# First row tiles of three feed-forward networks as block products, two opened side by side

## The chip, the cores and the metric

The kernel runs on one core of one Trainium2 chip. The metric is the device time of one execution in microseconds (us), the median of several. The engines are TensorE (PE; its weight loads are listed as PEld and overlap the matmuls), VectorE (DVE), ScalarE (ACT), GpSimd (POOL) and SyncE (SP). Matrix products land in PSUM banks; everything else lies in on-chip tiles that DMA fills from memory. SP issues plain loads; POOL issues DMAs that add to what is already in the tile ("accumulate").

## The reference

A trunk of two layers over 512 frames and 16 meta tokens, 528 columns of 1024 channels in float32. Each layer has a feed-forward network, a mixer (attention and a convolution branch), and a second feed-forward network:

```python
def swiglu(x, w_gate, w_up, w_down):
    return (jax.nn.silu(x @ w_gate) * (x @ w_up)) @ w_down

for l in range(DEPTH):                       # DEPTH = 2, D_MODEL = 1024, D_FF = 2816
    h = h + 0.5 * swiglu(rmsnorm(h, ffn1_norm[l]), ffn1_w_gate[l], ffn1_w_up[l], ffn1_w_down[l])
    h = h + hybrid_mixer(rmsnorm(h, mix_norm[l]), ...)
    h = h + 0.5 * swiglu(rmsnorm(h, ffn2_norm[l]), ffn2_w_gate[l], ffn2_w_up[l], ffn2_w_down[l])
return rmsnorm(h, final_norm)[:, N_META:]
```

So there are four feed-forward networks, called here (layer, which): (0,0), (0,1), (1,0), (1,1). In each, gate and up are 22 row tiles of 128 channels.

## The kernel before

**Precision.** Each float32 operand is split into a high part (a cast) and a low part (the rest); a product is three matmuls: high x high, high weight x low, low weight x high. `split` (L76 to L80) does it: a ScalarE copy and a VectorE subtraction. For the mixer's weights (`MIXER`, L223 to L226) the low part is made otherwise: ScalarE writes -1 times the high part, and a POOL DMA accumulates the weight on it.

**Columns.** The 528 columns are two halves of 264. A *plain* tile (L492) computes one row tile of gate or of up: 8 channel tiles, 3 products, 2 halves, 48 matmuls.

**Block products.** `quad` (L566) computes two row tiles, m and m+1, of gate and up together. Weights are 2 by 2 blocks of channels and row tiles, the input 2 by 2 blocks of channels and column halves; seven block products of 24 matmuls take the place of eight. Four use sums of weight blocks: s1 = w11 + w12, s3 = w22 + w12, s2 = s1 + w22, s4 = s2 + w21 (s2 and s4 are added up in s1's tile); the other three use w11, w21 and w22 as they are. Their order is `QUAD` (L109). In it ScalarE copies the w11 product to a second bank (B) and the s1 product to a tile q, s2 adds into B, VectorE writes "the opposite" q - B to a bank E (L608), w21 finishes the first result, s3 adds into B, VectorE writes q - B again (c22), w22 finishes E, s4 finishes B. A result leaves in three steps: VectorE times the norm, ScalarE's Silu, VectorE times up; then `parts` splits it to ah and al for the down products. Sums of the input (sh, sl) are made by `sums` (L365).

**A network** (L467) begins with its *head* (L517): plain tiles of gate and up for m = 0, then m = 1, with the matmuls of the RMS norm and the last sums of the input after 12 matmuls of the second. Then come a quad for m = 2, 3, the first down products, more quads, and so on (`GROUPS`). The network (0,0) has its own head with four plain rows. Heads begin at 730.48, 1087.56 and 1793.79 us.

**Weights.** `units` (L130) lists them in the order of use. Each is loaded by SP into one of three buffers wr (`fetch`, L179), then made to a high and a low part wh and wl (four buffers each) three units ahead of its use (`LOOK`, `prep_unit`, L213). Block sums s1 and s3 are loaded by SP and completed by a POOL accumulate of w12, in two buffers each (`fetch_sums`, L196).

**Order.** Each engine works through its own queue in order. The framework's scheduler sets that order from the program's text and from priorities; code in `priority(n)` is moved, and a manual dependency puts one instruction behind another.

## Time and profile before

| | |
|---|---|
| time, median of 3 runs | 2152.31 us (2151.03 to 2152.36) |
| profiled execution, first to last instruction | 2150.5 us |
| TensorE busy | 2135.9 us (99%) |
| VectorE, ScalarE, GpSimd busy | 1521.5, 1137.9, 488.7 us |
| the SP queue, the accumulating queue | 226.36 MB, 95.44 MB |
| granted TensorE clock, mean | 0.999 |
| the 192 matmuls and 4 of the norm in head (1,0) | 1087.56 to 1111.43 us |

The profile is that of one execution. A row of a timeline has the start, the duration, the engine, the line of the program, the operation with its output and inputs by the program's names, and in brackets how long the engine had been idle before it and what released it. The chain follows the work that ended last back to its beginning; "PE pb L502 x48" there is 48 matmuls of line 502 into a tile pb.

### The profile page before, as it was taken

Reading aid. Unit: us, or ns where it says so; the run is one execution under the profiler, and the core shown is the slowest. Engines: PE = TensorE matmul, PEld = TensorE weight load, DVE = VectorE, ACT = ScalarE, POOL = GpSimd, SP = SyncE. Lnnn points to the kernel's source line nnn. Section 1 sums busy time; section 2 is a strip of 40 time slices with the busy share of each in tenths; the row PEclk is TensorE's granted clock in tenths of the full one; section 3 lists DMA queues with packets and bytes.
Section 4 is the critical chain, followed back from the end, with each engine's and each line's share of the span. In section 5 each row is a group of like instructions: output and inputs, shape, how many; then the busy total and the mean of one; then the engine's idle time right before and its main releaser. Section 6 shows DMA issues by size and latency. Waiting matters only on the chain.

```text
span 2150.5 us, 39932 instructions
## 1 busy us (share of the span) xinstructions
PE 2135.9 (99%) x16226; PEld 2052.8 (95%) x16226; DVE 1521.5 (71%) x2091; ACT 1137.9 (53%) x1587; POOL 488.7 (23%) x449
## 2 busy tenths in 40 slices
PE   9999999999999999999999999999999999999998
PEld 9999999999999999999999999999888889999897
DVE  7867685677766777677877676856677767767685
ACT  6434355467776545343554443554778775444354
POOL 1322321211111131313113223212112111322320
PEclk9999999999999999999999999999999999999999
DMA  8465536865578747464365655368656886665542
GB/s 236 133 165 141 142 104 198 181 138 119 134 169 180 175 129 189 129 161 122 99 169 145 168 140 146 103 193 184 142 127 133 187 188 167 159 175 143 144 111 77
DMA packets 140168, 324.90 MB, mean 151 GB/s; under 512 B 15568, under 2 KB 19664, under 8 KB 139984
## 3 DMA queue, kind: packets, MB, share of 16 engines
q1 hardware_dynamic: 101856, 226.36, 33.3%
q0 software_dynamic: 37440, 95.44, 26.1%
q8 instruction: 127, 2.08, 0.4%
q10 hardware_dynamic: 688, 0.55, 0.1%
q14 instruction: 57, 0.47, 0.1%
HBM read 315.86 MB, written 6.42 MB: 150 GB/s over the span
## 4 chain that ended last, share of the span: by engine, by line
PE 99%; ACT 0%; DVE 0%; DMA 0%; issue 0%; DVEq 0%; ACTq 0%
PE pb L580 16%; PE ps L580 16%; PE ps L720 15%; PE ps L260 12%; PE ps L706 10%; PE pe L260 6%; PE pb L260 6%; PE pe L580 5%; PE z L706 2%; PE ps L502 2%; PE pe L502 1%; PE pb L502 1%; PE z L877 1%; PE po L921 1%; PE z L900 1%; PE ps L554 1%
## 5 line engine op out<-in xcount | busy, mean ns | idle before, releaser
L79 ACT CAST wh<-wr 128x1024 fp32r<-128x1024 f32 (+4 forms) x275 | 242.2, 887 | 372.4 <-PE ps L260 94.5
L80 DVE TENSOR_TENSOR wl<-wr,wh 128x1024 fp32r<-128x1024 f32 (+4 forms) x275 | 300.6, 1096 | 57.4 <-ACT wh L79 53.5
L79 ACT CAST wh<-s 128x1024 fp32r<-128x1024 f32 x158 | 165.8, 1049 | 274.9 <-DVE s L236 83.1
L80 DVE TENSOR_TENSOR wl<-s,wh 128x1024 fp32r<-128x1024 f32 x158 | 216.1, 1368 | 59.4 <-ACT wh L79 58.7
L720 PE MATMUL ps<-uh,wh 128*128 128x264 f32 (+1 forms) x792 | 243.8, 308 | 0.0
L720 PE MATMUL ps<-uh,wl 128*128 128x264 f32 (+1 forms) x792 | 240.0, 303 | 0.0
L720 PE MATMUL ps<-ul,wh 128*128 128x264 f32 (+1 forms) x792 | 239.9, 303 | 0.0
L640 POOL TENSOR_TENSOR h<-h,dt 128x528 f32<-128x528 f32 (+1 forms) x96 | 179.9, 1879 | 258.1 <-DVE dt L638 255.2
L210 POOL DMA_DIRECT2D s<-wg x78 | 72.8, 938 | 596.9 <-DMA s<-wg 337.9
L748 DVE SCALAR_TENSOR_TENSOR y<-uc,prm,y 128x528 f32<-128x528 f32 (+1 forms) x240 | 197.7, 824 | 4.1
L224 ACT CAST wh<-wr 128x1024 fp32r<-128x1024 f32 x104 | 109.1, 1049 | 141.2 <-issue 46.9
L580 PE MATMUL ps<-ul,wh 128*128 128x264 f32 (+1 forms) x624 | 177.4, 284 | 0.0
L580 PE MATMUL pb<-sl,wh 128*128 128x264 f32 (+1 forms) x624 | 176.9, 283 | 0.0
L580 PE MATMUL ps<-uh,wl 128*128 128x264 f32 (+1 forms) x624 | 176.9, 283 | 0.0
L580 PE MATMUL pb<-sh,wl 128*128 128x264 f32 (+1 forms) x624 | 176.8, 283 | 0.0
L580 PE MATMUL pb<-sh,wh 128*128 128x264 f32 (+1 forms) x624 | 176.5, 283 | 0.0
L580 PE MATMUL ps<-uh,wh 128*128 128x264 f32 (+1 forms) x624 | 176.2, 282 | 0.0
L720 PEld LDWEIGHTS ps<-uh,wl 128*128 128x128 f32 x792 | 149.1, 188 | 5.9
L720 PEld LDWEIGHTS ps<-uh,wh 128*128 128x128 f32 x792 | 148.9, 188 | 5.4
L720 PEld LDWEIGHTS ps<-ul,wh 128*128 128x128 f32 x792 | 149.0, 188 | 5.1
L260 PE MATMUL ps<-ah,wh 128*128 128x264 f32 (+1 forms) x616 | 142.0, 300 | 0.0
L260 PE MATMUL ps<-ah,wl 128*128 128x264 f32 (+1 forms) x616 | 141.8, 300 | 0.0
(319 smaller groups left out, 6460.8 us busy)
## 6 DMA issues: line engine op xcount, KB each, us to landing
wr<-wd SPq DMA_DIRECT2D x96, 384.0 KB, 3.6
wr<-win SPq DMA_DIRECT2D x72, 512.0 KB, 4.4
wl<-win POOLq DMA_DIRECT2D x72, 512.0 KB, 7.8
wr<-wg SPq DMA_DIRECT2D x117, 256.0 KB, 3.0
wr<-wu SPq DMA_DIRECT2D x117, 256.0 KB, 3.4
s<-wg SPq DMA_DIRECT2D x78, 256.0 KB, 5.2
s<-wu SPq DMA_DIRECT2D x78, 256.0 KB, 5.7
s<-wg POOLq DMA_DIRECT2D x78, 256.0 KB, 5.2
```

The source lines that it names most:

```text
L79: act.copy(hi, x)
L80: dve.tensor_tensor(out=lo, in0=x, in1=f(hi), op=ALU.subtract)
L210: pool.dma_start(t[:, a:b], src, accum_op=ALU.add)
L224: act.copy(hi[:, :nk], raw[:, :nk])
L260: pe.matmul(ps[:, c, :n], wt[:, k0 + k, :], xt[:, s:s + n], start=(k == 0 and pi == 0), stop=(k == end and pi == 2))
L502: pe.matmul(ps[:, e, :TH], wt[:, k, :], xt[:, s], start=(k == ORDER[0] and pi == 0), stop=(k == ORDER[-1] and pi == 2))
L554: pe.matmul(ps[:, e, :TH], wt[:, k, :], xt[:, s], start=(k == 0 and pi == 0), stop=(k == KD - 1 and pi == 2))
L580: pe.matmul(ps[:, e, :TH], wt[:, 4 * e + kk, :], xt, start=start and kk == 0 and pi == 0, stop=kk == 3 and pi == 2, skip_group_check=True)
L640: pool.tensor_tensor(out=tri(h[j], mode), in0=tri(h[j], mode), in1=tri(t, mode), op=ALU.add)
L706: pe.matmul(ps, wt[:, k0 + k, :], xt[:, s], start=(n == 0 and pi == 0), stop=(n == nk - 1 and pi == 2))
L720: pe.matmul(ps, wt[:, k, :], xt[:, s], start=(n == 0 and pi == 0), stop=(n == KD - 1 and pi == 2))
L748: t = dve.scalar_tensor_tensor(out=y, in0=uc[i][:, c0 + k:k + T], scalar=col(w0 + k), in1=y, op0=ALU.mult, op1=ALU.add)
```

## The change

In the networks (0,1), (1,0) and (1,1) the plain tiles of m = 0 and 1 and the quad of m = 2 and 3 are replaced by `pair`: two block products, a for m = 0, 1 and b for m = 2, 3, side by side in the order `OPENING`. It begins with o11 of both (the product that a quad calls w11), which need no sums of the input, each with its first three channel tiles first; after them the norm's matmuls and o21a, then s1a, s2a, o21b, w22a, s3a, s1b, s4a, s2b, s3b, w22b, s4b. The order of the matmuls inside a head is as written; that of the other engines is the scheduler's, with `URGENT` for the PSUM copies. The "opposite" is done in two halves. The low parts of o11a, o11b and o21a are made as in the mixer, with a -1 copy and a POOL accumulate. s1a is loaded into a wr buffer and completed there. The network (0,0) and all quads but those three are as before, apart from `evict`, which has the same instructions as before.

```diff
+    RAW_OF = {"w11": (0, 0), "w22": (1, 1), "w12": (0, 1), "w21": (1, 0),
+              "o11": (0, 0), "o21": (1, 0)}
+    OPEN = ("o11", "o21")
+    OPENING = (("o11", 0), ("o11", 1), ("o21", 0), ("s1", 0), ("s2", 0), ("o21", 1), ("w22", 0), ("s3", 0), ("s1", 1),
+               ("s4", 0), ("s2", 1), ("s3", 1), ("w22", 1), ("s4", 1))
...
+    def open_pair(of, srcs):
+        ats = [(*of, src[2]) for src in srcs]
+        opened.update(ats)
+        return [((n, *ats[e]), srcs[e], n) for n, e in OPENING]
...
-            m = PLAIN if l or fi else PLAIN_FIRST
-            for m in range(m):
-                units += [((f"g{fi}", l, m), wg[l, m], 8), ((f"u{fi}", l, m), wu[l, m], 8)]
-            m += 1
+            if l or fi:
+                units += open_pair((fi, l), [(wg[l], wu[l], m) for m in (0, 2)])
+            else:
+                for m in range(PLAIN_FIRST):
+                    units += [((f"g{fi}", l, m), wg[l, m], 8), ((f"u{fi}", l, m), wu[l, m], 8)]
+            m = PLAIN_FIRST
...
-            fetches += [n, n + 5, n + 3]
+            later_sums.append((n, ("s1", "s3")))
+            fetches += [(n, (name, *at), name) for name in ("w11", "w22", "w21")]
+        elif nk == "s1" and at in opened:
+            first = units[n - 1][2] in OPEN
+            later_sums.append((n, ("s3",) if first else ("s1", "s3")))
+            fetches += [(n, key, nk)] if first else []
+        elif at in opened and nk in ("s2", "s4"):
+            fetches.append((n, ("w22" if nk == "s2" else "w21", *at), "w22" if nk == "s2" else "w21"))
         elif nk not in QUAD:
-            fetches.append(n)
+            fetches.append((n, key, nk))
+    def load(raw, n, *blocks):
+        for queue, block, kw in zip((nc.sync, pool), blocks, ({}, {"accum_op": ALU.add})):
+            for a, b, src in pieces(n, block):
+                queue.dma_start(raw[:, a:b], src, **kw)
...
+            load(raw, n, *(("w11", "w12") if block == "s1" else (block,)))
...
+        n, names = later_sums[min(state["sums"], len(later_sums) - 1)]
+        _, *at = units[n][0]
+        if state["sums"] == len(later_sums) or tuple(at[:2]) != quads["of"]:
             return
-        state["sums"] = n + 1
-        _, *at = units[n][0]
-        for name, first in (("s1", "w11"), ("s3", "w22")):
-            t = quads["pool"].tile([P, 8, P], F32, tag=name, bufs=2, name=name)
-            for a, b, src in pieces(n, first):
-                nc.sync.dma_start(t[:, a:b], src)
-            for a, b, src in pieces(n, "w12"):
-                pool.dma_start(t[:, a:b], src, accum_op=ALU.add)
+        state["sums"] += 1
+        for name in names:
+            bufs = 1 if name == "s1" and at[0] == 2 else 2
+            t = quads["pool"].tile([P, 8, P], F32, tag=name, bufs=bufs, name=name)
+            load(t, n, "w11" if name == "s1" else "w22", "w12")
...
-            raw = raws.pop(key)
-            if key[0] in MIXER:
+            raw, nk0, nk = raws[key], nk, 8 if nk in OPEN else nk
+            if key[0] in MIXER or nk0 == "o11" or nk0 == "o21" and units[n - 1][2] == "o11":
                 act.copy(hi[:, :nk], raw[:, :nk])
                 act.activation(lo[:, :nk], raw[:, :nk], AF.Copy, scale=-1.0)
-                pool.dma_start(lo[:, :nk], src[:, :nk].bitcast(F32R), accum_op=ALU.add)
+                for a, b, src in pieces(n):
+                    pool.dma_start(lo[:, a:b], src.bitcast(F32R), accum_op=ALU.add)
...
+            i = split(raws[("s1" if nk in ("s2", "s4") else nk, *at)], hi, lo)
+            if nk == "s3" and at in opened:
+                tc.add_manual_dep(i.ins, state["rsqrt"].ins.name, NOSYNC, reason="behind the norm")
...
+            i = split(r, hi, lo)
+            if behind:
+                tc.add_manual_dep(i.ins, behind.ins.name, NOSYNC, reason="behind the copies")
...
+    def pair(ptile, sp, st, mode, of, ats, between, take, done):
+        TH = (T if mode == FULL else SEQ) // 2
+        toks = halves(mode)
+        KH = KD // 2
+        def v(t):
+            return t[:, :, :TH]
+        def x(t, k):
+            return [tuple(p[:, toks[t]] for p in st["u"][kk + 4 * k]) for kk in range(KH)]
+        def sx(i):
+            return [tuple(p[:, i % 2] for p in st["S"][kk][i // 2]) for kk in range(KH)]
+        def products(ps, w, xs, start=False, ks=range(KH)):
+            hi, lo = w
+            for e in range(2):
+                for kk in ks:
+                    xh, xl = xs[kk]
+                    for pi, (wt, xt) in enumerate(((hi, xh), (hi, xl), (lo, xh))):
+                        pe.matmul(ps[:, e, :TH], wt[:, 4 * e + kk, :], xt, start=start and kk == 0 and pi == 0,
+                                  stop=kk == KH - 1 and pi == 2, skip_group_check=True)
+        def kept(c):
+            t = sp.tile([P, 2, TH], F32, tag="q", bufs=2, name="q")
+            with priority(-URGENT):
+                copies.append(act.copy(t, v(c)))
+            return t
+        def begin(c, t):
+            with priority(-URGENT):
+                copies.append(act.copy(v(c), t))
+        copies = []
+        def opposite(out, c, q):
+            for e in range(2):
+                with priority(-URGENT):
+                    dve.scalar_tensor_tensor(out=out[:, e, :TH], in0=c[:, e, :TH], scalar=-1.0, in1=q[:, e],
+                                             op0=ALU.mult, op1=ALU.add)
+        As = [ptile() for _ in range(2)]
+        ws = [unit("o11", *of, at) for at in ats]
+        for ks in (range(KH - 1), (KH - 1,)):
+            for A, w in zip(As, ws):
+                products(A, w, x(0, 0), True, ks)
+        Bs = [ptile("pb")]
+        begin(Bs[0], v(As[0]))
+        between(ptile("pe"), copies[0])
+        Bs.append(kept(As[1]))
+        q, E, c22 = {}, {}, {}
+        def step(name, n):
+            w = unit(name, *of, ats[n])
+            if name == "o21":
+                products(As[n], w, x(0, 1))
+                take(n, As[n], 0, 0)
+            elif name == "s1":
+                G = ptile() if n else ptile("pe")
+                products(G, w, sx(0), True)
+                q[n] = kept(G)
+            elif name == "s2":
+                if n:
+                    keep, Bs[n] = Bs[n], ptile()
+                    begin(Bs[n], keep)
+                products(Bs[n], w, sx(1))
+                E[n] = ptile("pe")
+                opposite(E[n], Bs[n], q[n])
+            elif name == "s3":
+                products(Bs[n], w, sx(2))
+                c22[n] = sp.tile([P, 2, TH], F32, tag="c22", bufs=2, name="c22")
+                opposite(c22[n], Bs[n], q[n])
+                take(n, c22[n], 1, 1)
+            elif name == "w22":
+                products(E[n], w, sx(3))
+                take(n, E[n], 1, 0)
+            else:
+                done(n, 1)
+                products(Bs[n], w, x(1, 1))
+                take(n, Bs[n], 0, 1)
+                done(n, 0)
+        for name, n in OPENING[2:]:
+            step(name, n)
...
+            def evict(g, u, c, t):
+                s = toks[t]
+                dve.tensor_tensor(out=g[:, s], in0=c[:, 0, :TH], in1=norm["r"][:, s], op=ALU.mult)
+                fn(g[:, s], g[:, s], AF.Silu)
+                dve.tensor_tensor(out=u[:, s], in0=c[:, 1, :TH], in1=g[:, s], op=ALU.mult)
...
-                pu, pn = ptile(), ptile("pe")
-                pg = plain("pb", "g", 0)
-                def between():
-                    norm["r"] = rms_rstd(fp, st, pn, mode)
-                    sums(gtile, 3, st, mode)
-                plain(pu, "u", 0, between)
-                evac(0, pg[:, :, :TH], pu[:, :, :TH])
-                pg = plain("ps", "g", 1)
-                evac(1, pg[:, :, :TH], plain("pe", "u", 1)[:, :, :TH])
+                ms = (0, 2)
+                gu = {}
+                def between(pn, behind):
+                    with priority(-URGENT):
+                        norm["r"] = rms_rstd(fp, st, pn, mode)
+                    sums(gtile, 3, st, mode, behind)
+                def take(n, c, i, t):
+                    if (n, i) not in gu:
+                        gu[n, i] = gtile(), fp.tile([P, T], F32, tag="up", bufs=3, name="up")
+                    evict(*gu[n, i], c[:, :, :TH], t)
+                def done(n, i):
+                    u = gu[n, i][1]
+                    if i:
+                        while late:
+                            parts(*late.pop())
+                        parts(u, ms[n] + 1)
+                    else:
+                        late.append((u, ms[n]))
+                with tc.manual_schedule(engines={mybir.EngineType.PE}):
+                    pair(ptile, quads["pool"], st, mode, (fi, l), ms, between, take, done)
```

TensorE, between s2 and s3 of a block product, network (0,1). Names: sh, sl sums of the input, uh, ul the input, wh, wl weights; ps, pb, pe banks. Before (s2 into pb, then the first rows of w21; 24 of these stand ahead of s3, which is again into pb):

```order
L580 MATMUL pb<-sl,wh 128x264
L580 MATMUL pb<-sh,wl 128x264
L580 MATMUL ps<-uh_8436,wh 128x264
L580 MATMUL ps<-ul_8437,wh 128x264
L580 MATMUL ps<-uh_8436,wl 128x264 [waits DVE_49]
```

With the change, at s2b and s3b:

```order
L440 MATMUL ps<-sl,wh 128x264
L440 MATMUL ps<-sh,wl 128x264
L293 MATMUL ps<-ah,wh 128x264 [waits Activation_49]
L293 MATMUL ps<-ah,wh 128x264
L293 MATMUL ps<-al,wh 128x264 [waits DVE_49]
L293 MATMUL ps<-al,wh 128x264
L440 MATMUL ps<-sh,wh 128x264 [waits DVE_49]
L440 MATMUL ps<-sl,wh 128x264
```

Between the last matmul of s2 and the first of s3 there stood 24 of w21; now there are four of a down tile (L293), and s3b's first one waits for VectorE.

VectorE at the same place: the instructions from s2's result on, before and then with the change (q - B is L608 before, L458 after):

```order
L608 SCALAR_TENSOR_TENSOR pe<-pb,q 128x2x264 [waits PE_49,Activation_49]
L80 TENSOR_TENSOR wl<-s_8902,wh 128x1024 [waits Activation_49]
L592 TENSOR_TENSOR g<-ps,rstd 128x264 [waits PE_49]
L80 TENSOR_TENSOR wl<-wr,wh 128x512 [waits DMAHW7_49,Activation_49]
L594 TENSOR_TENSOR up<-ps,g 128x264 [waits Activation_49]
```

```order
L645 TENSOR_TENSOR up<-pb,g 128x264 [waits Activation_49]
L458 SCALAR_TENSOR_TENSOR pe<-ps,q 128x264 [waits PE_49]
L81 TENSOR_TENSOR al<-up,ah 128x528 [waits Activation_49]
L458 SCALAR_TENSOR_TENSOR pe<-ps,q 128x264 [waits DVE_49]
L81 TENSOR_TENSOR wl<-wr,wh 128x512 [waits DMAHW1_49,Activation_49]
```

One instruction has become two halves, and a split (al) that waits for ScalarE stands between them. At s2a (bank pb) it is an addition of weights that waits for a load (L268).

ScalarE, from the opening of the same head to the block sums. Before (rstd is the norm, s_8902 a block sum):

```order
L79 CAST wh<-wr 128x1024 [waits DMAHW2_49,DMAHW1_49,PE_49]
L103 ACTIVATE rstd<-pe,bias 128x528 [waits PE_49]
L103 ACTIVATE rstd<-rstd,bias 128x528 [waits Activation_49]
L99 ACT_TABLE_LOAD
L79 CAST wh<-s_8902 128x1024 [waits DMASW1_49,DMASW0_49,PE_49]
L103 ACTIVATE g<-g 128x528 [waits DVE_49]
```

With the change:

```order
L80 CAST wh<-wr 128x1024 [waits DVE_49,PE_49]
L451 COPY pb<-ps 128x2x264 [waits PE_49]
L105 ACTIVATE rstd<-pe,bias 128x528 [waits PE_49]
L446 COPY q<-ps 128x528
L105 ACTIVATE rstd<-rstd,bias 128x528 [waits Activation_49]
L80 CAST sh<-g 128x528 [waits DVE_49]
L80 CAST wh<-wr 128x1024 [waits DMAHW7_49,DMAHW0_49]
L80 CAST sh<-g 128x528 [waits DVE_49]
L101 ACT_TABLE_LOAD
L80 CAST wh<-wr 128x1024 [waits DMAHW6_49,DMAHW5_49,PE_49]
L80 CAST wh<-s_8914 128x1024 [waits DMASW1_49,DMASW0_49,PE_49]
L446 COPY q<-pe 128x528 [waits PE_49]
```

The first row is now the cast of s2a, and the copy of the bank (L451) stands behind it; the copy of s1a's product to q (the last row) stands behind the cast of a block sum, s3a's, that waits for an accumulate (DMASW).

55 lines of the change are left out of this document (25 added, 30 removed).

## The prediction

> **What bounds the kernel now.** I read the page's first and fourth parts first, then the table of TensorE's waits. Columns of the waits: engine, tile and line, who released it, us in total, times, longest.
>
> ```profile
> span 2150.5 us, 39932 instructions
> PE 2135.9 (99%) x16226; PEld 2052.8 (95%) x16226; DVE 1521.5 (71%) x2091; ACT 1137.9 (53%) x1587; POOL 488.7 (23%) x449
> PE 99%; ACT 0%; DVE 0%; DMA 0%; issue 0%; DVEq 0%; ACTq 0%
> ...
> PE ps L554 <- ACT wh L79: 4.8, 1, 4.8
> PE z L924 <- ACT vb L862: 0.2, 1, 0.2
> ```
>
> TensorE is the bound: 99% of the chain is its matmuls, and it waited twice, 4.8 us at the very start and 0.2 us in the mixer. So a matmul left out is worth its full time, and a stall that the new order brings costs its full time; no cover is left on this engine. The other engines matter by when they deliver. The three heads, in the chain in order of time (start us, duration us, what):
>
> ```profile
> 730.48 5.85 PE pb L502 x48
> ...
> 737.79 0.49 PE pe L409 x4
> ...
> 1087.56 5.83 PE pb L502 x48
> ...
> 1117.27 2.94 PE pb L580 x24
> 1120.21 2.90 PE ps L580 x24
> ...
> 1131.93 0.12 PE ps L260
> ...
> 1793.79 5.66 PE pb L502 x48
> ```
>
> H is the start of a head: 730.48, 1087.56, 1793.79. Today a head (4 plain tiles and a quad, 360 matmuls, and 4 for the norm) runs without a gap: 1131.93 - 1087.56 = 44.4 us. In the quad L580 each product of 24 goes to another tile than the one before it, so that what follows a product on the other engines has 2.9 us of cover.
>
> **The gain.** 14 products of 24 are 336 matmuls against 360: 24 fewer in each head, 72 in all. One matmul: 5.85/48 and 5.83/48 = 0.122 us, 5.66/48 = 0.118 us. 24 of them: 2.92 + 2.92 + 2.83 = **8.7 us**, 0.40% of the time. It's the only gain; everything below is subtracted from it.
>
> **Stalls that the new order has in it.** Four places, each from a chain of instructions that the trace has under other lines. Columns: start, duration, engine, line, operation, [idle before, releaser].
>
> ```profile
> 730.39 0.77 DVE L1078 TENSOR_TENSOR h<-ps,h 128x264 f32<-128x264 f32 x2 [1.90 <-PE ps L706]
> ...
> 1094.16 0.49 DVE L377 SCALAR_TENSOR_TENSOR g<-h,prm,g 128x264 f32<-128x264 f32 x1
> 1094.57 1.22 DVE L80 TENSOR_TENSOR wl<-wr,wh 128x1024 fp32r<-128x1024 f32 x1
> ...
> 1114.05 1.22 DVE L80 TENSOR_TENSOR wl<-wr,wh 128x1024 fp32r<-128x1024 f32 x1
> 1115.18 0.70 DVE L80 TENSOR_TENSOR al<-up,ah 128x528 fp32r<-128x528 f32 x1
> 1115.80 1.22 DVE L80 TENSOR_TENSOR wl<-s,wh 128x1024 fp32r<-128x1024 f32 x1
> ...
> 1120.32 0.72 DVE L608 SCALAR_TENSOR_TENSOR pe<-pb,q 128x528 f32<-128x528 f32 x1 [0.79 <-PE pb L580]
> ...
> 1123.15 0.43 DVE L592 TENSOR_TENSOR g<-ps,rstd 128x264 f32<-128x264 f32 x1 [0.67 <-PE ps L580]
> 1123.69 0.69 DVE L80 TENSOR_TENSOR wl<-wr,wh 128x512 fp32r<-128x512 f32 x1
> 1124.30 0.43 DVE L594 TENSOR_TENSOR up<-ps,g 128x264 f32<-128x264 f32 x1
> ...
> 1117.23 1.05 ACT L79 CAST wh<-wr 128x1024 fp32r<-128x1024 f32 x1 [0.98 <-ACT pb L599]
> 1118.18 0.59 ACT L603 COPY q<-ps 128x528 f32<-128x528 f32 x1
> 1120.18 1.05 ACT L79 CAST wh<-s 128x1024 fp32r<-128x1024 f32 x1 [1.41 <-PE pb L580]
> ```
>
> (1) s3b, every head. The product s3b adds into the bank from which "opposite" of s2b still reads, and s2b is the product right ahead of it; between them PE has four matmuls of the first down tile. Today w21's 24 stand there. The chain: s2b's end to VectorE 0.11 (1120.32 against 1120.21); a half of "opposite" 0.45 (the 128x264 row at L377 lasts 0.49, and the next begins 0.41 after it); the split al that the order puts between the halves 0.62 (pitch of 1115.18 to 1115.80); the second half 0.45; back to PE 0.1 (as on the way there). 1.73 us, less 4 x 0.122: **1.25 us**.
>
> (2) o21a, every head. It waits for ScalarE's copy of the bank (pb<-ps, L451). Ahead of that copy in ScalarE's queue stands s2a's cast, and it waits for the matmul before the last of o11a (its wh buffer). So after o11a's end: cast 0.95 (pitch of 1117.23 to 1118.18), copy 0.59, hand-overs 2 x 0.1 = 1.74, against 6 matmuls of o11b and 4 of the norm, 1.22: **0.5 us**.
>
> (3) Bank of the second down tile, every head. It is s4b's bank, free when the last evict has read it. Today's evict reads it 1124.30 + 0.43 - 1123.11 = 1.62 us after its product, VectorE's cast of a weight in between; with 0.1 and less the first tile's 12 matmuls, 1.46: **0.3 us**. Today that tile has a bank that was freed long before.
>
> (4) o11a, head (0,1) alone. Its bank is now that of the last output tile of the mixer, which VectorE reads until 730.39 + 0.77 = 731.16; with 0.1 that is **0.8 us** after H. Today the first product takes pb. The other two heads take a bank that is free.
>
> The sum: 2.85, 2.05 and 2.05, **6.95 us**. Bounds: from 1, if the orders of the other queues come out kinder than I read them and only the bank of (4) is left, to 10.3, if in one head of the three each of (1) to (3) meets one more 128x1024 split (3 x 1.13). I take 6.95, since the durations are those of the trace and the orders are those of the built program.
>
> **Loads and casts that come later than needed.** The transfers by queue (packets, MB, share of 16 engines' span), the stretches around two heads (stretch; busy PE, PEld, DVE, ACT, POOL; PEclk, DMA share, GB/s) and the first waits on them:
>
> ```profile
> q1 hardware_dynamic: 101856, 226.36, 33.3%
> q0 software_dynamic: 37440, 95.44, 26.1%
> ...
> 715.00:730.50 15.50, 15.50 (x129) 15.50 (x128) 11.76 (x20) 7.10 (x12) 0.00 (x0) 1.00 0.35 111
> 730.50:754.00 23.50, 23.50 (x195) 23.50 (x195) 16.77 (x24) 12.11 (x17) 7.10 (x8) 1.00 0.87 212
> ...
> 1076.00:1087.60 11.60, 11.60 (x97) 11.60 (x96) 11.56 (x19) 7.73 (x13) 0.00 (x0) 1.00 0.39 121
> 1087.60:1111.00 23.40, 23.40 (x194) 23.40 (x193) 16.79 (x25) 12.35 (x18) 7.04 (x8) 1.00 0.88 219
> 1111.00:1132.00 21.00, 21.00 (x174) 21.00 (x173) 14.85 (x22) 10.05 (x16) 3.50 (x4) 1.00 0.56 136
> ...
> 1091.53 0.33 SPq L208 DMA_DIRECT2D s<-wg  x1
> ...
> 1097.21 0.88 POOL L210 DMA_DIRECT2D s<-wg  x1 [40.06 <-DVE sl L80]
> ...
> 1105.80 1.05 ACT L79 CAST wh<-s 128x1024 fp32r<-128x1024 f32 x1 [7.66 <-DMA s<-wu]
> ```
>
> Prices, for here and below: SP's queue 226.36 MB in 0.333 x 2150.5 us = 316 GB/s of all engines, POOL's accumulating one 95.44 MB in 0.261 x 2150.5 = 170 GB/s. A head now moves 3 more units of 512 KB on SP (1.57 MB, 5.0 us) and 5 more on POOL (three lower parts and one more pair of sums with w12; 2.62 MB, 15.4 us): 20.4 us of all engines. The trace has room in the stretches ahead and inside: in head (1,0) 0.61 x 11.6 + 0.12 x 23.4 + 0.44 x 21 = 19.1 us. It's nearly all taken, and nothing of it is free in the middle stretch. SP has 10 and POOL 10 more issues in each head, 0.3 to 0.9 us each by the rows above; neither is busy on its own account, but they stand in line.
>
> (5) w22a, head (1,0). The block sums can't be issued before VectorE's nsum frees their place: SP issues from 1091.53, POOL's accumulate from 1097.21, and the sum s was cast only at 1105.80, after ScalarE had waited 7.66 us for it. Now w22a starts at H + 5.83 + 0.49 + 4 x 2.92 = 1105.6 and needs "opposite" of s2a, which needs q of s1a, which stands on ScalarE behind the cast of s3a, the one that waits for that landing. The chain after the landing: cast 0.95, copy 0.59, two halves 0.9, s4a's add between them 1.13, hand-overs 0.4: 4.0 us. s3a is now the first sum of its group, as s1 was today, and the group has three sums, not four (s1a goes ahead through a buffer of the ordinary weights). It lands between 1102.7 (one accumulate of a sum less beside it, 0.524 MB at 170 GB/s, 3.1 us) and today's 1105.8, and w22a is ready between 1106.7 and 1109.8: a stall of 1.1 to 4.2 us, and of none if the queues serve it first. I take **2.0**, the middle of none and the latest.
>
> (6) VectorE, head (1,0). All it does in a head, 15 passes of 128x1024 at 1.13 (1114.05 to 1115.18), 14 of 528 at 0.62, 28 of 264 at 0.41 and 4 of 512 at 0.61 (1123.69 to 1124.30), is 40 us of 42: from nothing to one pass, 1.1 us, behind (5). **0.8**.
>
> (7) The same in heads (0,1) and (1,1), where the place of the sums is free when the head begins and the loads go 6 us sooner: 0 to 0.6 each, **0.6** together.
>
> **The sum.** The profiled execution has 2150.5 us from first to last instruction; the median of the runs is 2152.3, 1.8 more, and I take the same around it after. -8.7 + 6.95 + 2.0 + 0.8 + 0.6 = +1.7: 2152.2 in the span, **2154.0 us** as a time. A measurement of this kernel can tell about 0.2%, 4.3 us; so my forecast is no measurable difference, with the gain paid back in small gaps. Its own range is 2148.0 to 2156.6.
>
> **Rivals.**
>
> *The waits hide (faster).* PE's stalls (1), (2) and (3) hang on the order in queues that have idle time (ScalarE 12.35 of 23.4 us busy). If the copies and halves get through ahead of the casts, 8.7 - 6.95 becomes 8.7 less 1 to 2 us (2152.3 - 8.7 + 1 to 2): 2144.6 to 2145.6. For it: no wait in any quad today. Against it: today's quads have a product between each reader and writer of a bank, and (1) hasn't.
>
> *Transfers decide (slower).* One mechanism: up to H + 23.4 a head must land 18.8 us more of the transfers above (three lower parts at 3.1 each, 9.3; the second block's sums 2 x 3.1 + 2 x 1.65 = 9.5), and has room for 7.1 + 2.8 = 9.9 in head (1,0), 10.1 + 3.1 = 13.1 in head (0,1), taken for (1,1) too: 8.9, 5.7 and 5.7 us short, 20 in all. PE takes what the weights that lie ready (three units, 8.8 us a head) don't cover. Where half gets through it is 10 us in place of the 3.4 of (5) to (7): 2160.6. It decides from about a quarter (5 us) on. For it: 0.88 in the middle stretch and ScalarE's 7.66 us. Against it: with 0.88 PE waited for nothing.
>
> *The clock drops at a gap (slower).* The program's first matmuls, and its last stretches, where PE ends:
>
> ```profile
> 4.83 3.18 PE ps L554 x12
> ...
> 14.52 1.46 PE ps L554 x12
> ...
> 2140.00:2145.00 5.00, 1.05 (x4) 0.30 (x2) 4.23 (x9) 1.78 (x4) 0.00 (x0) 0.93 0.61 201
> 2145.00:2150.50 5.50, 0.00 (x0) 0.00 (x0) 1.11 (x2) 0.00 (x0) 0.00 (x0) 0.50 0.58 192
> ```
>
> The first 12 matmuls, after the 4.8 us wait, took 3.18 us, later ones 1.46: 1.7 us lost on top of the gap. At the end PE stops at about 2141.05, and a mean of 0.93 over 5 us, where the level after is 0.50, means that the clock fell 0.7 us before 2145: 3.2 us after PE's stop. If each head had a gap of that length, the forecast would be 3 x 1.7 = 5.1 later: 2159.1. For it: the upper bound of (5), 4.2 us. Against it: all my other gaps are under 1.3. The Trainium skill, "TensorE: Matmul & The Clock Gate", "What's actually happening", has the clock at half after an idle window of about 3.4 us, and "Why this matters for your kernels" there asks for no gap above about 3 us between bursts of matmuls. The trace's 3.2 agrees; by that rule gaps of 1.3 us cost only themselves, and only (5) at its worst pays more.
>
> *That it doesn't do what it says* is excluded: the built program has 72 matmuls fewer.
>
> **Chances.** Forecast (between 2148.0 and 2156.6) 0.54; hidden waits 0.14; transfers 0.26; clock 0.06. Faster by more than 0.2%: 0.14; within: 0.54; slower: 0.32. The range is **2147 to 2163**: it cuts the far half of the first rival (0.07) and what lies past two thirds of the transfers' price (0.08).
>
> **What would show it.** Right: PE's waits name s3b on VectorE (1.2 us, three times), o21 on ScalarE (0.5), o11 in head (0,1) on VectorE (0.8), w22 in head (1,0) the longest; a head lasts 42 to 44 us. If the waits on PE in the three heads sum to under 4 us, the first rival has it; if the longest are released by a DMA, or by a cast that waited for one, in all three heads, the second. A PEclk below 1.00 inside a head would be the third. The prediction is wrong at its root if time is lost outside the heads: then something that I took to be unchanged (the mixer's end, the quads behind) has moved.

## The result: slower, outside the range

The changed kernel takes 2169.5 us, median of 5 runs (2168.14 to 2170.83), against 2152.28 before: 1.0082 times, 95% interval 1.007 to 1.0094. That is 17 us slower, where the prediction said 2154.0 (2147 to 2163). One run of `e1_one` below took 3468.73 us, at a mean granted clock of 0.556, and is left out of its median. The profiled execution has 2169.1 us in its span, 18.6 more than before. The page of the changed kernel:

```profile
PE 2136.9 (99%) x16154; PEld 2050.3 (95%) x16154; DVE 1532.5 (71%) x2127; ACT 1159.5 (53%) x1620; POOL 515.9 (24%) x479
```

and TensorE's waits in it, all but one of 0.2 us in the mixer:

```profile
PE pe L440 <- DVE pe L458: 12.8, 3, 4.6
PE ps L698 <- ACT wh L80: 4.9, 1, 4.9
PE ps L293 <- ACT wh L80: 2.7, 3, 0.9
PE ps L440 <- ACT pb L451: 0.9, 3, 0.3
PE ps L440 <- ACT wh L80: 0.8, 1, 0.8
PE ps L440 <- DMA wl<-wu: 0.6, 1, 0.6
PE ps L440 <- DMA wl<-wg: 0.3, 1, 0.3
```

TensorE has 72 matmuls fewer and is busy 1 us longer. The first wait of the list is new: w22a waits for the bank E ("opposite"), once in each head. Where the time lies is seen in three stretches, from the first matmul of a head to the first of the quad m = 4, by their windows (columns as in the prediction). Before:

```profile
730.32:798.07 67.75, 67.75 (x558) 67.75 (x557) 45.34 (x62) 29.02 (x41) 22.85 (x19) 1.00 0.65 164
1087.39:1155.18 67.79, 67.79 (x558) 67.79 (x557) 46.49 (x65) 29.73 (x43) 22.80 (x19) 1.00 0.64 168
1793.63:1858.74 65.11, 65.11 (x460) 60.88 (x459) 45.43 (x60) 28.39 (x41) 21.00 (x19) 1.00 0.67 171
```

and changed:

```profile
731.36:804.60 73.24, 67.50 (x533) 66.64 (x533) 51.52 (x75) 32.48 (x49) 24.64 (x21) 0.98 0.73 187
1093.77:1168.75 74.98, 69.13 (x534) 67.89 (x533) 52.91 (x78) 33.55 (x50) 24.60 (x21) 0.95 0.78 197
1807.03:1877.76 70.73, 64.96 (x436) 59.66 (x435) 51.50 (x75) 33.18 (x49) 24.17 (x21) 0.98 0.78 203
```

The three took 200.65 us and take 218.95: 18.3 of the 18.6 us. Outside them 0.3 us came on in sum, and o11a's wait of 0.84 us in head (0,1) is part of that, since it ends where the first stretch begins. Before, TensorE had no gap in them. By the count of matmuls they should have come down to 200.65 - 8.67 = 192.0. Now TensorE is idle in them for 218.95 - 201.59 = 17.4 us, and its busy time is 9.6 us above 192.0. Of that the mean clock explains 0.02 x 73.24 + 0.05 x 74.98 + 0.02 x 70.73 = 6.6 us. The other 3 are not the clock: `e13_dd` below, whose clock is at 1.00 in all three stretches, has them too (65.15 + 66.05 + 63.67 = 194.87). They may be the edges of the gaps, since a matmul's row lasts 0.28 us while the next begins 0.12 us later, so that the last one before a gap counts for more; this is not shown.

The mechanism, in the changed kernel's timeline of SP and of VectorE in head (0,1):

```profile
743.06 0.33 SPq L208 DMA_DIRECT2D wr<-wg  x1
743.43 1.24 SPq L208 DMA_DIRECT2D wr<-wu  x1
...
747.28 0.44 DVE L458 SCALAR_TENSOR_TENSOR pe<-pb,q 128x264 f32<-128x264 f32 x1
752.98 1.23 DVE L268 TENSOR_TENSOR wr<-wr 128x1024 f32<-128x1024 f32 x1 [5.26 <-DMA wr<-wu]
754.12 0.43 DVE L458 SCALAR_TENSOR_TENSOR pe<-pb,q 128x264 f32<-128x264 f32 x1
```

and that load in its list of DMA issues (KB, us to landing):

```profile
wr<-wu SPq DMA_DIRECT2D x1, 256.0 KB, 9.5
```

The two halves of E stand 6.8 us apart. Between them VectorE waits 5.26 us for w21a, the summand of s4a, which TensorE needs only three products after w22a. E's second half could have run at 747.7; TensorE was at work on o21b until 750.1, so w22a would have followed without a gap. In the heads (1,0) and (1,1) the addition stands and waits in the same place:

```profile
1115.92 1.23 DVE L268 TENSOR_TENSOR wr<-wr 128x1024 f32<-128x1024 f32 x1 [2.19 <-DMA wr<-wu]
...
1828.12 1.23 DVE L268 TENSOR_TENSOR wr<-wr 128x1024 f32<-128x1024 f32 x1 [4.01 <-DMA wr<-wu]
```

What follows the gap is slow as well. The chain in head (0,1):

```profile
754.70 4.69 PE pe L440 x24
759.39 2.93 PE pb L440 x24
```

and windows behind the three gaps:

```profile
754.10:759.40 5.30, 4.70 (x26) 4.73 (x27) 4.53 (x7) 1.53 (x3) 1.76 (x2) 0.68 0.81 191
1117.06:1123.26 6.20, 5.62 (x25) 5.65 (x26) 4.60 (x7) 1.60 (x3) 0.84 (x2) 0.50 0.99 283
1829.00:1834.50 5.50, 4.67 (x26) 4.70 (x27) 4.47 (x7) 1.57 (x3) 0.11 (x1) 0.69 0.88 280
```

The granted clock is 0.50 to 0.69 on average in these windows. In the trace it falls to 0.50 for 3.41 us in the heads (0,1) and (1,1) and for twice that in (1,0). The 24 matmuls behind the gaps take 4.69, 5.62 and 4.60 us in place of 2.92, 2.92 and 2.83, 6.2 us more in all.

### The profile page after: what moved, and what is told of

It is laid out like the page before. It is cut to its first block, busy times and chain, and to the rows that moved or that the text cites. A ratio compares the mean times of both kernels' runs of the same rounds, so it can differ in the third digit from the quotient of the medians.

```text
span 2169.1 us, 39993 instructions
## 1 busy us (share of the span) xinstructions
PE 2136.9 (99%) x16154; PEld 2050.3 (95%) x16154; DVE 1532.5 (71%) x2127; ACT 1159.5 (53%) x1620; POOL 515.9 (24%) x479
## 4 chain that ended last, share of the span: by engine, by line
PE 94%; DMA 3%; DVE 1%; ACT 1%; issue 0%; POOL 0%; SPq 0%; DVEq 0%; ACTq 0%; POOLq 0%
PE ps L858 15%; PE pb L722 14%; PE ps L722 14%; PE ps L293 12%; PE ps L844 9%; PE pe L293 5%; PE pb L293 5%; PE pe L722 5%; PE z L844 2%; PE ps L440 1%; DMA wr<-wu 1%; PE pe L440 1%; PE z L1015 1%; PE po L1059 1%; PE z L1038 1%; PE pb L440 1%
## 5 line engine op out<-in xcount | busy, mean ns | idle before, releaser
L81 DVE TENSOR_TENSOR wl<-wr,wh 128x1024 fp32r<-128x1024 f32 (+4 forms) x272 | 295.8, 1090 | 55.4 <-ACT wh L80 52.0
L81 DVE TENSOR_TENSOR wl<-s,wh 128x1024 fp32r<-128x1024 f32 x161 | 220.8, 1371 | 47.0 <-ACT wh L80 46.1
L858 PE MATMUL ps<-uh,wh 128*128 128x264 f32 (+1 forms) x792 | 243.8, 308 | 0.0
L858 PE MATMUL ps<-uh,wl 128*128 128x264 f32 (+1 forms) x792 | 240.0, 303 | 0.0
L858 PE MATMUL ps<-ul,wh 128*128 128x264 f32 (+1 forms) x792 | 239.9, 303 | 0.0
L255 ACT CAST wh<-wr 128x1024 fp32r<-128x1024 f32 x113 | 118.6, 1049 | 146.0 <-issue 50.4
L722 PE MATMUL ps<-ul,wh 128*128 128x264 f32 (+1 forms) x576 | 163.7, 284 | 0.0
L722 PE MATMUL pb<-sl,wh 128*128 128x264 f32 (+1 forms) x576 | 163.3, 284 | 0.0
L722 PE MATMUL ps<-uh,wl 128*128 128x264 f32 (+1 forms) x576 | 163.2, 283 | 0.0
L722 PE MATMUL pb<-sh,wl 128*128 128x264 f32 (+1 forms) x576 | 163.2, 283 | 0.0
L722 PE MATMUL pb<-sh,wh 128*128 128x264 f32 (+1 forms) x576 | 162.9, 283 | 0.0
L722 PE MATMUL ps<-uh,wh 128*128 128x264 f32 (+1 forms) x576 | 162.6, 282 | 0.0
L293 PE MATMUL ps<-ah,wh 128*128 128x264 f32 (+1 forms) x616 | 142.5, 301 | 2.7 <-ACT wh L80 2.7
L293 PE MATMUL ps<-al,wh 128*128 128x264 f32 (+1 forms) x616 | 141.8, 300 | 0.0
```

What stands on the lines that cost most here:

```text
L81: dve.tensor_tensor(out=lo, in0=x, in1=f(hi), op=ALU.subtract)
L255: act.copy(hi[:, :nk], raw[:, :nk])
L293: pe.matmul(ps[:, c, :n], wt[:, k0 + k, :], xt[:, s:s + n], start=(k == 0 and pi == 0), stop=(k == end and pi == 2))
L722: pe.matmul(ps[:, e, :TH], wt[:, 4 * e + kk, :], xt, start=start and kk == 0 and pi == 0, stop=kk == 3 and pi == 2, skip_group_check=True)
L858: pe.matmul(ps, wt[:, k, :], xt[:, s], start=(n == 0 and pi == 0), stop=(n == KD - 1 and pi == 2))
```

## The experiments

Two parts make the wait: an instruction for later work stands ahead of one that TensorE needs, and the load that it waits for comes late. The late load can be due to wr buffers (three; s1a holds one from its load until s4a's addition, so w21a's load waits for another) or to the number of transfers (the engines' share in head (0,1) is 1.00 to 1.11 from 725 to 750).

### The order on VectorE

`e1_one`: "opposite" in one instruction.

```diff
-            for e in range(2):
-                with priority(-URGENT):
-                    dve.scalar_tensor_tensor(out=out[:, e, :TH], in0=c[:, e, :TH], scalar=-1.0, in1=q[:, e], ...)
+            with priority(-URGENT):
+                dve.scalar_tensor_tensor(out=v(out), in0=v(c), scalar=-1.0, in1=q, ...)
```

> The changed kernel with each 'opposite' (q - B) written as one VectorE instruction in place of two halves; s4a's addition, which waits for w21a's load, can then no longer stand between the halves. Theory 1 (the order on VectorE: the second half of E for w22a waited behind that addition): the three waits of w22a (12.8 us, up to 4.6 each) go to under 0.5 each, and with them the slow 24 matmuls behind them (4.69, 5.62 and 4.60 us against 2.9, 6.2 us in all); s3b's wait shrinks too, since no split stands between halves (0.8 us a head). About 2149 us. Theory 2 (the transfers are too many: the load of w21a is late whatever the order): PE stalls as long, a product or two later, behind the same load: 2164 or more.

Measured: 2166.81 us, 1.0066 (1.0046 to 1.0086). Waits:

```profile
PE pb L440 <- DVE c L457: 6.4, 2, 3.6
...
PE pb L440 <- ACT q L446: 4.4, 1, 4.4
PE ps L440 <- DVE pe L457: 2.4, 3, 0.8
...
PE pe L440 <- DVE pe L457: 0.2, 1, 0.2
```

w22a no longer waits (0.2), and hardly anything is gained: the next to wait are s4a and its neighbours (pb), 10.8 us for c22a and q, which come on VectorE and ScalarE after the same late additions of weights.

`e3_behind`: halves kept; a dependency puts the addition behind the split of the unit before it.

```diff
-                dve.tensor_tensor(out=x, in0=x, in1=y, op=ALU.add)
+                i = dve.tensor_tensor(out=x, in0=x, in1=y, op=ALU.add)
+                if nk == "s4" and at in opened:
+                    tc.add_manual_dep(i.ins, state["lo"].ins.name, NOSYNC, reason="behind the unit before")
```

> The changed kernel, halves kept, with one dependency more that moves no transfer: s4a's (and s4b's) addition of weights is put behind the split of the unit before it, so both halves of E stand ahead of it on VectorE. Theory 1 (order): as with the single instruction for w22a, -12.2 us of waits and -6.2 of slow matmuls, s3b's wait stays: about 2151 us. Theory 2 (transfers): 2164 or more, the wait moved to s1b or s4a.

Measured: 2166.22 us, 1.0069 (1.0054 to 1.0084). The wait for E is gone here too, and again s4a waits, for c22a (8.1 us, 3 times, 4.0 at most). VectorE now stands at s4a's addition and then at s2b's for their loads (2.54 and 1.66 us in head (0,1)). Theory 1, that this one order is the whole loss, falls: mending it was worth 2.7 us in `e1_one` and 3.3 here, of 17. Both times lie where theory 2 put them, but whether transfers or buffers make the load late these two runs don't tell.

`e4_order`: with that dependency, s2b ahead of s4a.

```diff
-               ("s4", 0), ("s2", 1), ("s3", 1), ("w22", 1), ("s4", 1))
+               ("s2", 1), ("s4", 0), ("s3", 1), ("w22", 1), ("s4", 1))
```

> The kernel with that dependency, and the opening's order changed in one place: s2b ahead of s4a, so that 24 matmuls stand between s2b and s3b. Theory 1: s3b's wait goes, 1.25 us a head below the kernel with the dependency alone by the prediction's working, 0.9 by the after profile's longest wait there: about 2148 us, unless w22b, loaded one place sooner, comes late. Theory 2: as slow as the kernel with the dependency alone or slower.

Measured: 2156.57 us, 1.0023 (1.0014 to 1.0032), 9.7 below its parent; the edit was meant for 0.9 a head. The three stretches take 69.22, 70.93 and 66.24 us. It moves s4a, and with it the need for w21a, a product later, and w22b's load ahead of w21a's: it gives the late load more time, which the expectation had not thought of. With its parent's edit it takes off 12.9 of the 17 us, though no buffer is freed and no byte less is moved. So the loss needs both parts, a late load and an order that asks for it early, and mending either one takes off a part. The wait at s3b goes to 0.7 in one head; the copy into s2b's bank costs 3.9 in its place.

### Buffers or transfers

`e6_s2x`: s2a's sum in a tile of its own, so that s1a's wr buffer comes free early (c22 gets one buffer to make room).

```diff
+                z = x
+                if nk == "s2" and ("s1", *at) in counted:
+                    z = raws[("s1", *at)] = quads["pool"].tile([P, 8, P], F32, tag="s2x", bufs=1, name="s2x")
+                    state["out"] -= 1
+                    counted.remove(("s1", *at))
-                dve.tensor_tensor(out=x, in0=x, in1=y, op=ALU.add)
+                dve.tensor_tensor(out=z, in0=x, in1=y, op=ALU.add)
```

> The changed kernel with one edit for the buffers: s2a's sum is written to a tile of its own, not over s1a's, so s1a's wr buffer (one of three, held in the changed kernel from s1a until s4a's addition) comes free some ten us sooner, and w21a's load, issued in the changed kernel only when o21b's split frees a buffer (743.1), can go about 3 us sooner. c22 has one buffer in place of two to make room. Theory B (two wr buffers left in circulation make the loads late): w22a's waits fall from 12.8 us in all to 3 to 5, with the slow matmuls behind them: 2155 to 2158. Theory T (the transfer engines are full, share 1.06 there, so an earlier issue only shares them longer): waits fall by 3 or less, 2165 or more.

Measured: 2159.72 us, 1.0035 (1.0022 to 1.0048). SP, the addition and the halves in head (0,1):

```profile
734.76 0.33 SPq L208 DMA_DIRECT2D wr<-wg  x1
...
747.12 0.43 DVE L463 SCALAR_TENSOR_TENSOR pe<-pb,q 128x264 f32<-128x264 f32 x1
747.46 1.22 DVE L273 TENSOR_TENSOR s2x<-s2x,wr 128x1024 f32<-128x1024 f32 x1
748.59 0.43 DVE L463 SCALAR_TENSOR_TENSOR pe<-pb,q 128x264 f32<-128x264 f32 x1
```

w21a is loaded 8.3 us sooner (734.76 for 743.06). The addition still stands between the halves and waits for nothing; the stretch of head (0,1) is 66.87 us, 6.4 below the changed kernel's. Theory B holds, for that head altogether. In the other two w22a waits on, 3.7 and 2.9 us.

`e7_late` fetches the sums of the quad behind the head later, `e8_reuse` makes s1a in o11a's tile, `e5_split` makes the three low parts on VectorE, `e14_nolo` leaves them incomplete:

```diff
# e7_late
-            if nk == ("s1" if at in opened else "w11"):
+            if nk == ("w11" if at not in opened else "s1" if units[n - 1][2] in OPEN else "w22"):
                 fetch_sums()
# e8_reuse
+                raw = state.pop("o11") if block == "s1" else wpool.tile([P, 8, P], F32, tag="wr", bufs=RAW, name="wr")
+            if block == "s1":
+                for a, b, src in pieces(n, "w12"):
+                    pool.dma_start(raw[:, a:b], src, accum_op=ALU.add)
# e5_split
-            if key[0] in MIXER or nk0 == "o11" or nk0 == "o21" and units[n - 1][2] == "o11":
+            if key[0] in MIXER:
# e14_nolo
-                for a, b, src in pieces(n):
+                for a, b, src in pieces(n) if key[0] in MIXER else ():
                     pool.dma_start(lo[:, a:b], src.bitcast(F32R), accum_op=ALU.add)
```

> The changed kernel with one edit for the transfers: the block sums of the quad behind the head (m = 4: 1.05 MB on SP and 1.05 MB of accumulates) are fetched when w22b is prepared, not when s1b is, so that 9.5 us of all engines' time move out of the stretch in which w21a, w22b and the pair's own sums land. Theory T: waits on PE in the heads fall by half or more, with the slow matmuls: 2156 to 2160. Theory B: w21a is issued at the same time and stays late: 2166 or more.

> The changed kernel, with s1a made in o11a's own wr tile: the block w11 already lies there, so only w12's accumulate is issued, and 512 KB of SP loads (1.7 us of all engines) fall away in each head. Both theories: little, 2166 to 2170; nearer the first by theory T.

> The changed kernel, halves and order of the opposite kept, but the low parts of o11a, o11b and o21a made by VectorE's subtraction, so that three accumulates of 512 KB (9.2 us of all transfer engines) less run in each head. Theory 2 (transfers decide when w21a lands): the load lands in 3 to 4 us in place of 8, w22a's waits fall to under 1 us each and the time to about 2153. Theory 1 (the order alone): the wait stays where the load is issued late: 2163 to 2170.

> The changed kernel without the three accumulating DMAs (1.57 MB a head, 9.2 us of all transfer engines by the prices of the prediction) that complete the low parts of o11a, o11b and o21a: these low parts hold -1 times the high part, so the result is not the reference's. Nothing else changes on any engine, VectorE included. Theory B (w21a's load is issued when a wr buffer comes free, at 743): it lands a little sooner, the waits for E fall from 12.8 to 9 or more, 2163 or more. Theory T (the number of transfers): they fall to under 5, about 2157 or less.

Measured: `e7_late` 2168.72 (1.0076, 1.0059 to 1.0093), `e8_reuse` 2168.3 (1.0075, 1.006 to 1.009), `e5_split` 2166.0 (1.0065, 1.005 to 1.008), `e14_nolo` 2163.47 (1.0056, 1.0043 to 1.007). The waits for E, in this order without `e8_reuse` (12.2 us there):

```profile
PE pe L440 <- DVE pe L458: 11.1, 3, 4.0
```

```profile
PE pe L440 <- DVE pe L458: 6.7, 3, 3.9
...
PE pe L440 <- ACT sh L80: 1.6, 1, 1.6
PE pe L440 <- DVE sl L81: 1.3, 1, 1.3
```

```profile
PE pe L440 <- DVE pe L458: 10.0, 3, 4.5
```

With 1.57 MB a head less and nothing else touched, 6.0 us are gained; a buffer freed earlier, with the same bytes, gains 9.8. Moving 2.1 MB out of the head, or saving 0.5 MB, takes off 0.8 and 1.2 us, no more than the runs of one kernel scatter. By head, (0,1), (1,0) and (1,1), w22a waited 4.6, 3.7 and 4.5 us in the changed kernel; `e6_s2x` leaves 0, 3.7 and 2.9 and `e14_nolo` 1.6, 3.9 and 4.5. So in head (0,1) the late load is first one of buffers and second one of transfers, and theory T alone falls; in (1,0) neither edit shortens the wait. VectorE's subtractions in place of the accumulates halve the wait for E, but the sums of the input come late in head (1,0) (sh, sl) and the gain is 3.5.

### What comes next when that is mended

`e9_late_reuse_s2x` joins the edits of `e6_s2x`, `e7_late` and `e8_reuse`.

> The three edits of the buffers, the later sums and the reuse of o11a's tile together. If buffers and transfers each hold a part of the late loads, w22a's waits are gone (under 1 us in all), and what is left are the prediction's order stalls (s3b 0.9 a head, o21a 0.3, o11 0.8) against 8.7 of gain: about 2149. If the loads are late for another reason, 2160 or more.

Measured: 2158.24 us, 1.0031 (1.0019 to 1.0043), between the two cases. Head (0,1) is at 66.87; w22a waits 3.9 us in (1,0) and 2.3 in (1,1). ScalarE in head (1,0):

```profile
1104.79 1.05 ACT L80 CAST wh<-s 128x1024 fp32r<-128x1024 f32 x1 [5.16 <-DMA s<-wu]
1105.74 0.59 ACT L457 COPY q<-pe 128x528 f32<-128x528 f32 x1
```

This is point 5 of the prediction, chain and size: the copy to q stands behind the cast of s3a's sum, which lands late.

`e10_deps`: on `e6_s2x`, three dependencies; `e11_deps_order`: with s2b ahead of s4a and the copy into its bank written earlier; `e12_all`: with the reuse, and the banks of o11a and o11b exchanged.

```diff
# e10_deps: the split of s3a behind the copy to q and the second half of E, s4a's addition behind that half
+                    tc.add_manual_dep(i.ins, state.pop("kept").ins.name, NOSYNC, reason="behind the copy to q")
+                    tc.add_manual_dep(state["lo3"].ins, state["opp"].ins.name, NOSYNC, reason="behind the opposite")
+                if nk == "s4" and at in opened and "opp" in state:
+                    tc.add_manual_dep(i.ins, state["opp"].ins.name, NOSYNC, reason="behind the opposite")
# e11_deps_order: in the step of w22a, ahead of its products
+                if not n:
+                    keep, Bs[1] = Bs[1], ptile()
+                    begin(Bs[1], keep)
# e12_all
-        As = [ptile() for _ in range(2)]
+        As = [ptile() for _ in range(2)][::-1]
```

> The kernel with s2a's sum in a tile of its own, plus three dependencies that move no transfer: s3a's cast behind the copy of s1a's product to q (ScalarE), s3a's split behind the second half of E (VectorE), s4a's addition behind that half too. Its parent still waited 3.7 and 2.9 us for E in the heads (1,0) and (1,1). Theory Q (there the copy to q stands behind the cast of s3a's sum, which lands late: point 5 of the prediction): these waits go, and the slow 24 matmuls behind each with them: 2159.7 - 6.6 - 3.6, about 2149.5. Rival L (s3a's sum lands so late that s3a itself, 2.9 us further on, waits instead): 2153 to 2158.

> As the kernel with the three dependencies, and s2b ahead of s4a in the opening, with the copy into s2b's bank written one product sooner, so that 24 matmuls stand between s2b and s3b. Theory Q, and the prediction's point 1: 0.9 us less in each head, about 2147. If w22b, now needed sooner, lands late: 2150 or more.

> As the kernel with dependencies and order, plus s1a made in o11a's wr tile (512 KB of loads less in each head), and o11a and o11b with their banks exchanged, so that o11a in head (0,1) does not wait for VectorE's last read of the mixer's bank (0.84 us in the changed kernel, point 4). About 2145 to 2146.

Measured: 2159.15 (1.0034, 1.0021 to 1.0047), 2156.05 (1.0019, 1.0009 to 1.0028) and 2156.25 (1.0015, 1.0006 to 1.0025), 9 us and more above what theory Q expected of each. No wait for E above 0.4 us is left in any of them, and the gain is small: the wait has moved on. Of the first, then of the last:

```profile
PE pb L450 <- ACT ps L461: 4.0, 2, 2.6
PE ps L303 <- ACT wh L80: 3.8, 3, 2.0
```

```profile
PE ps L309 <- DVE up L665: 5.0, 3, 2.3
...
PE ps L456 <- ACT wh L80: 0.8, 1, 0.8
```

In the last kernel the heads' own products wait 3.0 us in sum, and the first down tiles 5.0, since the last eviction (up) stands on VectorE behind the split of a down weight that waits for its load (in head (0,1) ScalarE's cast of that weight waited 2.38 us for it). The exchange of banks took nothing off the 0.8 us of o11a.

`e13_dd`: `e12_all` without the exchange, the sums of `e7_late`, and the first down weights behind the eviction.

```diff
+                if key[0][0] == "d" and key[2] == 0 and (key[1] or key[0] == "d1"):
+                    for a, b in zip((i, state["lo"]), state["evict"]):
+                        tc.add_manual_dep(a.ins, b.ins.name, NOSYNC, reason="behind the evict")
```

> As the last kernel (s2a's sum in its own tile, the three dependencies, s2b ahead of s4a, s1a made in o11a's tile), without the exchange of banks, which took nothing off; the sums of the quad behind the head are fetched later; and the casts and splits of the first down weights stand behind the eviction emitted before them, since there the last eviction (up) waited behind a down weight's split for a load (5.0 us in the three heads, and a matmul clock of 0.66 behind it in (0,1)). Theory: every wait found so far was an instruction on ScalarE or VectorE that waits for a load with one behind it that PE needs sooner; with these gone too, 2 to 3 us of small waits are left against 8.7 of gain: 2146 to 2149. Rival (the loads themselves are too many for the head, so that PE waits for the next weight whatever the order): 2152 or more.

Measured: 2151.66 us, 0.9997 (0.9988 to 1.0006): no difference to the kernel before. The three stretches:

```profile
730.99:796.45 65.46, 65.15 (x532) 64.86 (x533) 51.58 (x75) 32.52 (x50) 24.44 (x21) 1.00 0.80 208
1085.63:1154.83 69.20, 66.05 (x534) 65.11 (x533) 52.60 (x78) 33.39 (x49) 24.53 (x21) 1.00 0.83 214
1793.15:1858.70 65.55, 63.67 (x436) 58.20 (x435) 51.38 (x75) 32.84 (x49) 22.79 (x21) 1.00 0.83 218
```

They sum to 200.2 us, 18.7 below the changed kernel and 0.4 below the kernel before. In head (0,1) the change is worth 67.75 - 65.46 = 2.3 of its 2.9 us inside the stretch; ahead of it o11a still waits 0.83 us, and the quad m = 4 begins 1.6 us earlier than before (796.45 for 798.07). (1,1) loses 0.4 by the change and (1,0) 1.4.

`e15_dd_nolo` leaves the low parts of `e13_dd` incomplete (the edit of `e14_nolo`); `e16_two` uses the opening in (0,1) and (1,1) alone:

```diff
+ASIS = ((0, 1),)
-            if l or fi:
+            if (l or fi) and (fi, l) not in ASIS:
-                (first_head if first else head)()
+                (first_head if first else plain_head if (fi, l) in ASIS else head)()
```

> The same left out (low parts of o11a, o11b, o21a hold -1 times the high part, the result is not the reference's) from the last kernel, in which buffers, orders and evictions are mended and 2150.4 in the span is left. If what keeps its head (1,0) at 69.2 us against 64.9 for its matmuls alone is the number of transfers, this head comes under 67 and the time to 2147 to 2149; if it is the place of the sums (they cannot be issued before nsum), 2150 or more.

> The last kernel, with the opening in the networks (0,1) and (1,1) alone; (1,0) begins with plain tiles and a quad as before the change. From its heads (65.5 and 65.6 us from the head's first matmul to the quad m = 4, against 67.8 and 65.1 before, and 69.2 in (1,0) against 67.8): 1.4 us below the last kernel, about 2150.2 as a time, 0.1% under the kernel before; at most 2149 if (1,1) comes out as in the best run of its parent, 64.4.

Measured: 2149.09 (0.9989, 0.998 to 0.9998) and 2152.42 (1.0003, 0.9994 to 1.0013). With fewer transfers head (1,0) is at 68.72, not under 67: its rest is hardly the number of these transfers; (1,1) falls from 65.55 to 63.21. That (1,0)'s rest is the place of its sums is the expectation's other case, and no run moved that place. `e16_two` gains nothing over its parent and misses its 2150.2. Its stretches sum to 198.2 us, 2.0 below the parent's, but it loses as much outside them; 1.1 of that is a wait just ahead of its plain head in (1,0), which the kernel before had not:

```profile
PE pb L649 <- DVE h L810: 1.1, 1, 1.1
```

No version beats the kernel before by more than can be measured with the whole result computed.

## Why the prediction was wrong

**The gain** of 8.7 us is there: 24 matmuls at 2.92 us fewer in each head, and head (0,1) of `e13_dd` shows 2.3 us of its share of 2.9, from which o11a's wait is still to be taken.

**Points 1 to 4**, the stalls in the order, came out somewhat below their size, 4.4 us for 6.95: 0.9 us a head for 1.25 between s2b and s3b, 0.3 for 0.5 at o21a, 0.8 for 0.8 at o11a, none seen for 0.3 at the second down tile. Two were right in place and not in cause, so that their sizes are in part luck. Between s2b and s3b it is the four down matmuls that wait, for a cast of a weight (wh) that stands on ScalarE behind the cast ah, by the chain:

```profile
769.16 1.23 DVE wl L81
770.39 0.35 DVE up L645
...
771.30 0.62 ACT wh L80
...
771.96 0.78 PE ps L293 x4
```

(the cast ah waits for the eviction up, and that stands behind a split again), so that one instruction for the "opposite" changed little there. And o11a's 0.8 did not go with another bank. The trace puts the wait to a cast of a weight on ScalarE that ends as o11a starts (730.31 + 1.04 = 731.35 for 731.36, and 730.11 for 730.11 in `e12_all`); VectorE's update of h had ended 0.15 us earlier. No run moved that cast.

**Points 5 to 7** are the step that failed: 3.4 us were set, and 12.8 us of waits and 6.2 of slow matmuls came. Point 5 put s4a's addition between the halves of E at its duration, 1.13 us, "s4a's add between them". The order showed that it waits for a load; I priced the instruction and not its wait. Had I asked when that load can be issued, I'd have found the buffers: with s1a in one of three until that very addition, w21a's load has to wait for o21b's split. The mechanism that I did follow, the cast of s3a's late sum ahead of the copy to q, exists. In head (1,0) of the changed kernel ScalarE waits 2.69 us for that sum, the copy to q begins at 1111.69 and E's first half at 1113.30; the wait for w21a comes behind that half and ends last. With w21a early it costs 3.9 us (`e9_late_reuse_s2x`; bounds 1.1 to 4.2). And points 5 and 7 held (0,1) and (1,1) to be safe, since their sums can be loaded sooner; the sums were not what was late.

**The rivals.** "Transfers decide" (2160.6, chance 0.26) had the direction and a part of the cause: transfers were worth 6.0 us in `e14_nolo`, the buffers 9.8 in `e6_s2x`, and the rival did not have them. "The clock drops at a gap" (0.06) came true in all three heads, at about the price given (1.7 us): 1.8 us in two of them and 2.7 in the third, though behind gaps that the forecast did not hold. The forecast kept the two apart, and here a long gap brought the slow clock with it each time. "The waits hide" needed all of `e13_dd`'s edits and got to the time before, not below it.

**The root** was tested too: outside the three stretches 0.3 us were lost in sum, with o11a's 0.84 in it, so the mixer and the quads behind have not moved.

## What to carry to other kernels

An instruction in an in-order queue costs the wait in it, not its duration: where a new order puts work for later ahead of what the bound engine needs next, ask when its load can be issued and who holds the buffer. When several engines are nearly full in one stretch, mending one wait shows the next; mended one after the other here, they paid back a loss of 17 us and reached no gain. A long gap on TensorE has to be priced with the slower matmuls behind it, here 1.8 to 2.7 us.

## What the runs showed beyond that

The clock does not go by the length of the last gap alone. In `e12_all` a gap of 1.78 us in head (0,1) was followed by half the clock; in `e6_s2x` one of 2.90 us in (1,1) was not. The first, in TensorE's timeline:

```profile
775.73 0.57 PE L309 MATMUL ps<-ah,wh 128*128 128x264 f32 x2 [1.78 <-DVE up L665]
```

In these traces a fall inside the heads lasts 3.41 us or twice that, and the times between falls are whole multiples of the same length (in the changed kernel 358.4 and 706.6 us at full clock, 105 and 207 times 3.413). Cut into stretches of that length, counted from a fall of the same trace, the first place looks like this:

```profile
772.64:776.05 3.41, 1.63 (x13) 1.41 (x13) 1.12 (x3) 1.28 (x3) 1.15 (x2) 1.00 0.78 138
776.05:779.46 3.41, 3.41 (x18) 3.41 (x17) 0.71 (x1) 0.30 (x1) 0.00 (x0) 0.50 0.54 134
```

and the second like this:

```profile
1815.79:1819.20 3.41, 2.06 (x18) 1.86 (x16) 1.95 (x4) 1.85 (x3) 0.86 (x1) 1.00 1.11 264
1819.20:1822.61 3.41, 1.85 (x15) 1.88 (x16) 2.77 (x4) 2.00 (x2) 0.00 (x0) 1.00 1.10 263
1822.61:1826.02 3.41, 3.41 (x31) 3.41 (x30) 3.41 (x6) 1.70 (x3) 0.00 (x0) 1.00 1.03 299
```

TensorE is idle for 3.41 - 1.63 = 1.78 us of one stretch in the first, and the next stretch runs at 0.50, which costs 1.7 us. In the second the longer gap lies across a border, with 1.35 us idle on one side and 1.56 on the other, and the clock stays at 1.00. In the 17 traces, counting stretches at full clock, none with up to 1.56 us idle between matmuls was followed by a fall and each with 1.97 or more was; of seven between 1.65 and 1.81, five were. So in this program about half of such a stretch was enough. This is read from where the falls lie; no run moved a gap to test it.

The Trainium skill, "TensorE: Matmul & The Clock Gate", "What's actually happening", says that the clock falls after an idle window of some 3.4 us and that the window runs free, so that the moment varies. The length of 3.41 us and the gaps of 3.7 to 4.6 us agree. The drop behind 1.78 us does not fit a full idle window, and the measurement decides: a gap under 2 us can cost the clock too.
